# Row sums from HBM: five loads instead of six for the last rows, and the end of the sum without a second wait

## The chip, the core and the metric

The kernel runs on one NeuronCore of a Trainium2 chip. Its time is the device time of one execution in microseconds (us), taken some times on the chip; the profile of one execution goes with it. All times and profiles that are compared here ran at the full clock (1.00).

Words used below: a load *lands* when its semaphore gets the sixteenth of its sixteen increments, one from each DMA engine. The *eighth load* is the last full one (it lands near 137.8 us); the program is the same up to it in both kernels. The *last load* is the last piece of the last row. *Issue* in a chain of waits is time in which the engine waited for nothing that the profile shows; DVE is VectorE, and DVEq and SPq are the queues of VectorE and SyncE, whose semaphore and DMA instructions do not count as busy. A *paired sum* is one VectorE instruction that adds the first half of a piece to its second half and accumulates the sums.

## The reference, cut to what matters

```python
def reference(x):            # x: (32, 512, 1024) float32
    return np.sum(x, axis=-1).astype(np.float32)
```

It reads 67.1 MB and writes 64 KB.

## The kernel before

Each of 128 partitions gets 112 rows of 1024 numbers, in seven loads of 16 rows (the first cut into 1 and 15), then 16 rows more. VectorE reduces the rows; ScalarE takes six rows of the seventh tile and half of the rows of the last block. The last block is loaded in six pieces, so that little work is left when the last bytes land.

```python
BLOCKS = (112, 16); G = 16; ACT_ROWS = 6; CUT = 576
...
    def pairs_dve(xt, a, b, first, acc):
        h = (a + b) // 2
        nc.vector.tensor_tensor_reduce(
            out=xt[:, a:h], in0=xt[:, a:h], in1=xt[:, h:b], scale=1.0, scalar=first,
            op0=ADD, op1=ADD, accum_out=acc,
        )
...
    cuts = [0, 8, 12, 14, 15]          # rows: 8, 4, 2, 1, then the last row in 576 + 448
    for i, k in zip(cuts, cuts[1:]):
        nc.sync.dma_start(out=xt[:, i * D : k * D], in_=x_b[:, (c + i) * D : (c + k) * D])
    last = 15 * D
    for i, k in ((0, CUT), (CUT, D)):
        nc.sync.dma_start(out=xt[:, last + i : last + k], in_=x_b[:, c * D + last + i : c * D + last + k])

    for i, k in zip(cuts[:3], cuts[1:4]):
        h = (k - i) // 2
        rows_dve(xt, res, i, h, c + i)
        rows_act(xt, res, i + h, h, c + i + h)
    rows_act(xt, res, 14, 1, c + 14)
    pairs_dve(xt, last, last + CUT, 0.0, part)
    pairs_dve(xt, last + CUT, last + D, part, res[:, c + 15 : c + 16])
    nc.sync.dma_start(out=out_b, in_=res)
```

The second paired sum starts from the first one's sum (`part`), so it waits for two things: its load and the carried sum. The first one waits for two things too: its load, and VectorE's own semaphore. So the wait that the prediction calls write-behind-write is one behind a read, long over; it still takes a second semaphore.

## Time and profile before

| | before |
|---|---|
| time, median of the first three runs | 162.29 us (162.26 to 162.44) |
| span of the profiled execution | 160.5 us |
| VectorE busy | 76% |
| DMA, mean over the span | 418 GB/s |
| from the landing of the seventh load to that of the eighth (8.39 MB) | 19.35 us, 434 GB/s |

Three parts of the page of before (the profiler's summary of one execution): the span, the main queue (packets, MB, share of sixteen engines' span), and the chain of work that ended last, by engine:

```profile
span 160.5 us, 118 instructions
...
q1 hardware_dynamic: 2160, 67.12, 97.3%
...
DMA 74%; DVE 22%; SPq 1%; issue 0%; DVEq 0%
```

The load queue is busy for 97% of the span. The Trainium skill, "DMA: Bandwidth & Descriptors", section "Where 436 GB/s comes from", puts the ceiling of the ports at 435 GB/s, sixteen of 27.2 GB/s; the 434 GB/s above agree. The same section says that for transfers between HBM and SBUF (the on-chip memory) the HBM side, about 358 GB/s a core, binds; here, in a program on one core, it did not. Nothing but the last microseconds can be gained by moving work. This is the end of the chain of waits of before (start us, length us, what):

```profile
118.20 38.90 DMA xt<-in_x_dram
157.10 0.03 issue
157.13 0.02 DVEq L57
157.15 0.09 issue
157.24 0.46 DVE xt L57
157.70 0.02 DVE part L57
157.72 0.05 issue
157.77 0.45 DVE xt L57
158.22 0.01 DVEq L114
```

The 576-element load lands at 157.10, but the first paired sum starts at 157.24. In between lies a semaphore instruction of VectorE's queue (DVEq) of 0.02 us. The second paired sum starts at 157.77; its load landed at 157.633 by the trace, so 0.134 us go by after the last byte. The first paired sum's accumulator read ends at 157.705, 0.062 us before. The timeline of VectorE in before has both (start us, length us, engine, line, operation, operands):

```profile
157.24 0.46 DVE L57 CUSTOM_DVE_ANT_0 xt<-xt 128x288 f32<-128x288 f32 x1 [0.93 <-DMA xt<-in_x_dram]
157.62 0.08 DVE L57 DVE_READ_ACCUMULATOR2_ANT part<- 128x1 f32 x1
157.77 0.45 DVE L57 CUSTOM_DVE_ANT_0 xt<-xt,part 128x224 f32<-128x224 f32 x1
```

### The profile page before, as it was taken

Reading aid. Unit: us, or ns where it says so; the run is one execution under the profiler, and the core shown is the slowest. Engines: PE = TensorE matmul, PEld = TensorE weight load, DVE = VectorE, ACT = ScalarE, POOL = GpSimd, SP = SyncE. Lnnn points to the kernel's source line nnn. Section 1 sums busy time; section 2 is a strip of 40 time slices with the busy share of each in tenths; the row PEclk is TensorE's granted clock in tenths of the full one; section 3 lists DMA queues with packets and bytes.
Section 4 is the critical chain, followed back from the end, with each engine's and each line's share of the span. In section 5 each row is a group of like instructions: output and inputs, shape, how many; then the busy total and the mean of one; then the engine's idle time right before and its main releaser. Section 6 shows DMA issues by size and latency. Waiting matters only on the chain.

```text
span 160.5 us, 118 instructions
## 1 busy us (share of the span) xinstructions
DVE 122.7 (76%) x14; ACT 16.0 (10%) x29; POOL 0.2 (0%) x4
## 2 busy tenths in 40 slices
DVE  0000059997799959999499994999949998699992
ACT  0000000000000000000000000000000000692892
POOL 0000000000000000000000000000000000000000
DMA  9979996996996996996996996996997998999991
GB/s 376 490 306 429 490 523 261 523 523 261 523 523 261 523 523 261 523 523 261 523 523 261 523 506 278 523 506 278 523 474 310 523 425 359 392 425 425 419 401 46
DMA packets 2304, 67.18 MB, mean 418 GB/s; under 512 B 512, under 2 KB 640, under 8 KB 1024
## 3 DMA queue, kind: packets, MB, share of 16 engines
q1 hardware_dynamic: 2160, 67.12, 97.3%
q10 hardware_dynamic: 144, 0.06, 0.1%
HBM read 67.11 MB, written 0.07 MB: 418 GB/s over the span
## 4 chain that ended last, share of the span: by engine, by line
DMA 74%; DVE 22%; SPq 1%; issue 0%; DVEq 0%
DMA xt<-in_x_dram 74%; DVE res L41 21%; SPq L93 1%; DVE xt L57 1%; DVEq L57 0%; DVE part L57 0%; DVEq L114 0%
## 5 line engine op out<-in xcount | busy, mean ns | idle before, releaser
L41 DVE TENSOR_REDUCE res<-xt 128x16 f32<-128x16384 f32 (+4 forms) x10 | 121.8, 12203 | 34.5 <-DMA xt<-in_x_dram 34.5
L49 ACT ACT_TABLE_LOAD x1 | 1.3, 1283 | 137.9 <-DMA xt<-in_x_dram 137.9
L49 ACT ACTIVATE xt<-xt 128x1024 f32<-128x1024 f32 x14 | 14.6, 1042 | 3.7 <-DVE res L41 3.7
L49 ACT ACTIVATION_READ_ACCUMULATOR xt<-xt 128x1 f32 x14 | 2.6, 186 | 0.0
L57 DVE CUSTOM_DVE_ANT_0 xt<-xt 128x288 f32<-128x288 f32 x1 | 0.5, 459 | 0.9 <-DMA xt<-in_x_dram 0.9
L57 DVE CUSTOM_DVE_ANT_0 xt<-xt,part 128x224 f32<-128x224 f32 x1 | 0.5, 452 | 0.1
L151 POOL MEMSET const-uint8-127<- 128x1 uint8 x1 | 0.1, 102 | 0.0
L151 POOL MEMSET const-bfloat16-1.0<- 128x1 bf16 x1 | 0.1, 101 | 0.0
L151 POOL MEMSET const-float32-0.0<- 128x1 f32 x1 | 0.1, 98 | 0.2 <-issue 0.2
L151 POOL MEMSET const-float32-1.0<- 128x1 f32 x1 | 0.1, 98 | 0.0
L57 DVE DVE_READ_ACCUMULATOR2_ANT res<- 128x1 f32 x1 | 0.1, 84 | 0.0
L57 DVE DVE_READ_ACCUMULATOR2_ANT part<- 128x1 f32 x1 | 0.1, 83 | 0.0
## 6 DMA issues: line engine op xcount, KB each, us to landing
xt<-in_x_dram SPq DMA_DIRECT2D x1, 7680.0 KB, 21.3
xt<-in_x_dram SPq DMA_DIRECT2D x1, 4096.0 KB, 31.1
xt<-in_x_dram SPq DMA_DIRECT2D x1, 2048.0 KB, 35.7
xt<-in_x_dram SPq DMA_DIRECT2D x2, 512.0 KB, 21.1
xt<-in_x_dram SPq DMA_DIRECT2D x1, 1024.0 KB, 37.8
xt<-in_x_dram SPq DMA_DIRECT2D x1, 288.0 KB, 38.9
xt<-in_x_dram SPq DMA_DIRECT2D x1, 224.0 KB, 38.9
xt<-in_x_dram SPq DMA_DIRECT2D x6, 40.8
```

The costliest lines, as they stand in the source:

```text
L41: nc.vector.tensor_reduce(out=res[:, c : c + n], in_=xt[:, j * D : (j + n) * D].rearrange("p (j d) -> p j d", d=D), axis=X, op=ADD,)
L49: nc.scalar.activation(out=v, in_=v, func=COPY, accum_out=acc)
L57: nc.vector.tensor_tensor_reduce(out=xt[:, a:h], in0=xt[:, a:h], in1=xt[:, h:b], scale=1.0, scalar=first, op0=ADD, op1=ADD, accum_out=acc,)
L93: nc.sync.dma_start(out=xt[:, i * D : k * D], in_=x_b[:, (c + i) * D : (c + k) * D])
L151: nc = _bacc.Bacc("TRN2", target_bir_lowering=False, num_devices=1)
```

## The change

Its intent: fewer loads at the end, the last row cut nearer its middle, and a last paired sum that starts as soon as its load lands. The products get tiles of their own, so that the first paired sum waits for its load alone; a copy of one column takes the wait for the carried sum, so that the last paired sum too waits for its load alone. The diff, cut to its core:

```diff
-ACT_ROWS = 6
-CUT = 576
+ACT_ROWS = 7
+CUT = 544
...
+    seen = rpool.tile([P, 1], F32, name="seen")
+    pairs = [rpool.tile([P, D // 2], F32, name=f"pairs{i}") for i in range(3)]
...
-            out=xt[:, a:h], in0=xt[:, a:h], in1=xt[:, h:b], scale=1.0, scalar=first,
+            out=pairs[:, 0 : h - a], in0=xt[:, a:h], in1=xt[:, h:b], scale=1.0, scalar=first,
...
-    cuts = [0, 8, 12, 14, 15]
+    cuts = [0, 9, 13, 15]
...
-    for i, k in zip(cuts[:3], cuts[1:4]):
+    for i, k in zip(cuts[:2], cuts[1:3]):
         h = (k - i) // 2
         rows_dve(xt, res, i, h, c + i)
-        rows_act(xt, res, i + h, h, c + i + h)
+        rows_act(xt, res, i + h, k - i - h, c + i + h)
+    pairs_dve(xt, 13 * D, 14 * D, 0.0, res[:, c + 13 : c + 14], pairs[2])
     rows_act(xt, res, 14, 1, c + 14)
-    pairs_dve(xt, last, last + CUT, 0.0, part)
-    pairs_dve(xt, last + CUT, last + D, part, res[:, c + 15 : c + 16])
+    pairs_dve(xt, last, last + CUT, 0.0, part, pairs[0])
+    nc.vector.tensor_copy(out=seen, in_=part)
+    pairs_dve(xt, last + CUT, last + D, part, res[:, c + 15 : c + 16], pairs[1])
```

That a copy may stand in for the wait rests on the Trainium skill, "VectorE: DVE Perf Modes", section "The DRAIN you can't avoid": a value read by the next VectorE instruction can be stale, and a semaphore or one intervening VectorE instruction removes that.

More of the change, by code (lines that the diff above doesn't have):

```diff
@@ L53, in rows_act, with pairs_dve @@
             sum_act(xt[:, (j + i) * D : (j + i + 1) * D], res[:, c + i : c + i + 1])
-    def pairs_dve(xt, a, b, first, acc):
+    def pairs_dve(xt, a, b, first, acc, pairs):
         h = (a + b) // 2
         nc.vector.tensor_tensor_reduce(
-            out=xt[:, a:h], in0=xt[:, a:h], in1=xt[:, h:b], scale=1.0, scalar=first,
+            out=pairs[:, 0 : h - a], in0=xt[:, a:h], in1=xt[:, h:b], scale=1.0, scalar=first,
             op0=ADD, op1=ADD, accum_out=acc,
@@ L118 @@
     sp = mybir.EngineType.SP
+    fn = tc.nc.m.functions[0]
     entry, body = None, None
-    for blk in tc.nc.m.functions[0].blocks:
+    for blk in fn.blocks:
         ops = [i for i in blk.instructions if i.engine == sp]
```

## The prediction

> **What bounds the kernel now.** The load stream. In the chain of waits, 74% of the 160.5 us span is DMA; the tile that landed at 118.47 and the one at 137.82 are 8.39 MB apart, 434 GB/s. That is the ceiling of 435 GB/s in the Trainium skill, "DMA: Bandwidth & Descriptors", section "Where 436 GB/s comes from", so this trace agrees and the first 137 us cannot move: the diff touches nothing there. Only what follows the last bytes, and small costs at the ends of the last loads, can change.
>
> **The tail before** (timeline, semaphore landings). Landings: 8 rows 147.53, 4 rows 152.43, 2 rows 155.05, one row 156.32, 576 elements 157.10, 448 elements 157.63. First paired sum 157.24 to 157.70, its accumulator read ends 157.71; second paired sum starts 157.77, read ends 158.23, output store issued 158.29, landed 159.71, end 160.5. From the second paired sum's start, 2.7 us are fixed. It starts 0.13 us after its data. Two things hold it equally: a separate semaphore instruction of 0.02 us in front of it (the instruction waits for two semaphores), after which 0.085 us pass, and the carried sum, 0.06 us after the read. A reduction that waits for one DMA semaphore alone starts 0.024 us after the landing (137.817 to 137.841).
>
> **What the change does.**
> 1. Tiles of their own for the products take the write-behind-write wait on VectorE from the first paired sum: it needs only its load, so no semaphore instruction, 0.024 instead of 0.138 us after landing.
> 2. The copy takes the wait for the carried sum; the last paired sum then waits only for its load. The copy adds about 0.06 to 0.1 us (estimate from the 0.083 us accumulator read, also 128x1), mostly while the last load is in flight.
> 3. Five loads, not six. At 0.43 MB/us the one-row load should take 1.22 us and took 1.27, the 576 one 0.69 and took 0.78: a boundary costs 0.05 to 0.09 us. One fewer moves the last landing about 0.05 us earlier, to 157.58.
> 4. Rebalancing: 9-row reduction 9.74 us instead of 10.82, ending 147.6; 9 rows land about 148.75 instead of 147.53. ScalarE's last row (landing near 156.27) ends about 157.45, before VectorE: not critical. The 512-element paired sum (estimate 0.69 us: 0.459 for 288 elements plus 224 at the reductions' 1.05 ns each) runs 156.3 to 157.0, just in time for the 544 load at 157.01. No critical time.
>
> **Sum.** First paired sum starts about 157.04, read ends 157.49, copy 157.55 to about 157.62; last load 157.58, last paired sum starts about 157.63 rather than 157.77. With 240 elements rather than 224 (+0.02 us) the gain is about 0.12 us: span 160.38, time 162.17 us. The three runs spread 0.18 us; the range allows for that.
>
> **What would show it right or wrong.** No semaphore instruction on VectorE's queue before the paired sums, except the copy's own wait; last landing 157.5 to 157.6; last paired sum within 0.08 us after it; output issue near 158.17. If the 512-element sum delays the first piece's, step 4 is critical after all.
>
> **What would make it wrong.** A copy of over 0.15 us; the cut at 544 elements (2176 bytes, no multiple of 256), which may slow the last load; a 512-element paired sum well over 0.7 us; a slower chip. None can reach 2% (3.2 us).
>
> Predicted 162.17 us, 8 in 10 between 161.95 and 162.32; faster by over 2%: 0.01, within 2%: 0.98, slower: 0.01.

## The result

The changed kernel took 162.38 us (median of 4 runs, 162.08 to 162.57) and before 162.37 us (median of 4, 162.26 to 162.58): a ratio of 0.9997 with a 95% interval of 0.9978 to 1.0016. A ratio here is the mean time of one kernel's runs over that of the other's runs of the same rounds, so it is not quite the ratio of the medians. The time lies outside the predicted range, and the gain of 0.12 us is not to be seen. All outputs are right.

The same three parts of the page of the changed kernel:

```profile
span 160.6 us, 119 instructions
...
q1 hardware_dynamic: 2016, 67.12, 97.2%
...
DMA 75%; DVE 23%; SPq 0%; issue 0%; DVEq 0%
```

There are 144 packets fewer, one load's worth: 128 of data and 16 semaphore writes. The end of the chain of waits of the changed kernel:

```profile
117.43 39.13 DMA xt<-in_x_dram
156.55 0.02 issue
156.58 0.69 DVE pairs L59
157.27 0.01 DVE res L59
157.28 0.41 DVE pairs L59
157.69 0.02 DVE part L59
157.71 0.02 issue
157.73 0.15 DVE seen L112
157.88 0.40 DVE pairs L59
158.28 0.01 DVEq L120
```

The semaphore instruction is gone. The chain now names the copy (`seen`), with its end at 157.88 us. The timeline of VectorE in the changed kernel shows that the last sum runs since 157.82:

```profile
157.25 0.44 DVE L59 CUSTOM_DVE_ANT_0 pairs<-xt 128x272 f32<-128x272 f32 x1
157.61 0.08 DVE L59 DVE_READ_ACCUMULATOR2_ANT part<- 128x1 f32 x1
157.73 0.15 DVE L112 COPY seen<-part 128x1 f32<-128x1 f32 x1
157.82 0.47 DVE L59 CUSTOM_DVE_ANT_0 pairs<-xt,part 128x240 f32<-128x240 f32 x1
```

The last load landed at 157.792, and the last paired sum starts at 157.817, 0.025 us later, as predicted. So the wait was gained, and yet the span is longer. Adding up the two profiles by pieces, from the records of the trace, tells where it went (us):

| piece | before | changed | difference |
|---|---|---|---|
| start to the landing of the first load | 3.609 | 3.793 | +0.184 |
| to the landing of the eighth load | 134.208 | 134.209 | +0.001 |
| to the landing of the last load | 19.816 | 19.790 | -0.026 |
| to the start of the last paired sum | 0.134 | 0.025 | -0.109 |
| to the end of its accumulator read | 0.460 | 0.475 | +0.015 |
| to the issue of the store | 0.065 | 0.064 | -0.001 |
| to the store's landing | 1.421 | 1.413 | -0.008 |
| to the end of the span | 0.814 | 0.876 | +0.062 |
| sum | 160.527 | 160.645 | +0.118 |

Three rows were not foreseen. The slowest DMA engine's share of the *first* load landed 0.184 us later, where the programs are the same, and the stream never made that up. The stream's own end gained less than expected. And the end of the program after the store's landing became longer by 0.062 us.

The last of these is visible in SyncE's final checks. Before it stops, SyncE waits for every semaphore of the program, in pairs, in a fixed order. DMAs get their eight semaphores in turn. Before has 16 DMAs and its store is the sixteenth; the changed kernel has 15. Starts of SyncE's checks, from the trace (us; the store's landing is in the row of its semaphore):

| check | before | changed |
|---|---|---|
| 103 | 158.691 | 158.755 |
| 104, 101 | 158.749 | 158.813 |
| 105, 100 | 158.811 | 158.875 |
| 106, 99 | 158.875 | 159.786 (store landed at 159.769) |
| 107, 102 | 159.730 (store landed at 159.713) | 159.848 |
| 108, with the first drain | 159.795 | 159.913 |

In before the store's semaphore is in the last pair. In the changed kernel one more pair follows the landing, and a check takes 0.062 us from start to start.

### The profile page after: what moved, and what is told of

Same layout as the page of the kernel before. It is cut to its first block, busy times and chain, and to the rows that moved or that the text cites. A ratio compares the mean times of both kernels' runs of the same rounds, so it can differ in the third digit from the quotient of the medians.

```text
span 160.6 us, 119 instructions
## 1 busy us (share of the span) xinstructions
DVE 121.5 (76%) x16; ACT 17.2 (11%) x31; POOL 0.2 (0%) x4
## 4 chain that ended last, share of the span: by engine, by line
DMA 75%; DVE 23%; SPq 0%; issue 0%; DVEq 0%
DMA xt<-in_x_dram 75%; DVE res L43 21%; DVE pairs L59 1%; SPq L95 0%; DVE seen L112 0%; DVE part L59 0%; DVE res L59 0%; DVEq L120 0%
## 5 line engine op out<-in xcount | busy, mean ns | idle before, releaser
L43 DVE TENSOR_REDUCE res<-xt 128x16 f32<-128x16384 f32 (+3 forms) x9 | 119.8, 13309 | 36.5 <-DMA xt<-in_x_dram 36.5
L51 ACT ACTIVATE xt<-xt 128x1024 f32<-128x1024 f32 x15 | 15.6, 1044 | 2.4 <-DMA xt<-in_x_dram 2.3
L59 DVE CUSTOM_DVE_ANT_0 pairs<-xt 128x512 f32<-128x512 f32 (+1 forms) x2 | 1.1, 567 | 0.2 <-DMA xt<-in_x_dram 0.2
L59 DVE CUSTOM_DVE_ANT_0 pairs<-xt,part 128x240 f32<-128x240 f32 x1 | 0.5, 468 | 0.0
```

Of the source, the lines that this page charges most:

```text
L43: nc.vector.tensor_reduce(out=res[:, c : c + n], in_=xt[:, j * D : (j + n) * D].rearrange("p (j d) -> p j d", d=D), axis=X, op=ADD,)
L51: nc.scalar.activation(out=v, in_=v, func=COPY, accum_out=acc)
L59: nc.vector.tensor_tensor_reduce(out=pairs[:, 0 : h - a], in0=xt[:, a:h], in1=xt[:, h:b], scale=1.0, scalar=first, op0=ADD, op1=ADD, accum ...
```

## The experiments

The theory after this first look has four parts. **A**: the late first landing is chance of one execution, and hides the gain in the times. **C**: the end lost 0.062 us to the turn of the semaphores. **Waits**: own tiles and copy are worth about 0.11 us. **F**: a load costs each engine a fixed amount, so five are cheaper than six. The rivals: **B** or **H**, the late start belongs to the changed kernel (B: every time by the same lag; H: on the whole); **D**, the end's length is chance; **E**, the waits gain nothing; **F2**, the stream gains by the cut, not by the number of loads.

### b_same, a_same: both kernels again

No edit.

> The kernel before, unchanged, timed against itself. Theory A (the 0.185 us by which the slowest DMA engine lands later, from the first load on, is chance of one execution): its times spread by 0.2 us or more, ratio 1.000 within 0.002; in the profile the gap from the first to the sixteenth landing of the 137.8 us load can be anything from 0.3 to 0.7 us; the paired sum still starts 0.13 us after the last landing, and the last load lands 19.82 us after the eighth. Rival B (the lag belongs to the changed kernel): the gap is 0.28 us again, as in the first profile of before.

> The changed kernel again. Theory A: the same local tail as in its first profile whatever the lag: last paired sum 0.025 us after the last landing, end of the span 0.88 us after the output store's landing against 0.82 in before; ratio to before near 0.9996 and not resolved from 1; the gap of first to sixteenth landing differs from the 0.695 us of its first profile. Rival B: the gap is 0.69 us again and the ratio is 1.000 for that reason.

Before against itself: 162.21 against 162.20 us, ratio 1.0000 (0.9988 to 1.0012). The changed kernel: 162.25 against 162.20 us, ratio 1.0000 (0.9988 to 1.0012). The sixteen runs of before, its eleven and the five of b_same, reach from 162.06 to 162.52 us, so one execution differs from the next by up to 0.46 us, several times the effect. The gap from the first to the sixteenth increment of the eighth load, 0.280 us in the first profile of before and 0.695 in that of the changed kernel, was 0.460 in b_same and 0.461 in a_same: B falls, and H is left for the last experiment. The Trainium skill, "DMA: Bandwidth & Descriptors", section "Why a DMA increments its semaphore by 16 and not by 1", says that the engines of one DMA finish independently; this is that, and the load is done when the slowest is.

In a_same the last paired sum again starts 0.024 us after the last landing and the end takes 0.875 us after the store's landing, so both local findings repeat. The time does not move by anything that can be resolved, as theory A expects (0.9996 lies within the interval); but its own mean was 0.01 us over that of before, so this alone shows no gain.

### a_out_last: the store's semaphore moved back by an extra load

```diff
-            parts = (0, 1, m) if done + c == 0 else (0, m)
+            parts = (0, 1, 8, m) if done + c == 0 else (0, m)
```

> The changed kernel with the first tile cut once more (rows 1 to 7 and 8 to 15), so that there are 16 transfers, as before, and the output store again has the semaphore that the end of the kernel checks last. Theory C (the end lost 0.062 us because another semaphore is checked after the store's): the end of the span comes 0.82 us after the store's landing, not 0.88, and from the last load's landing to the end it takes 2.79 us against 2.85 in the changed kernel and 2.90 in before. Rival D (the 0.06 us is chance of the end): still 0.88.

From the store's landing to the end it took 0.813 us, and from the last landing to the end 2.789, as theory C expects. The time was 162.15 against 162.20 us, ratio 0.9997 (0.9984 to 1.0011): no gain that can be resolved. The extra load is not free. A packet usually takes 8 to 9 ns beyond its bytes at the 27.2 GB/s of one port: 611 ns for 16,384 bytes (602 by the rate), 159 for 4,096 (151), 25 for 448 (16.5). A load has eight data packets and a semaphore write of 9 ns on each engine, so an estimate from these is 8 x 8.4 + 9 = 0.076 us for each additional load, and this edit pays that to gain 0.062.

### w_only: the waits alone, on the loads of before

```diff
+    seen = rpool.tile([P, 1], F32, name="seen")
+    pairs = [rpool.tile([P, D // 2], F32, name=f"pairs{i}") for i in range(2)]
...
-            out=xt[:, a:h], in0=xt[:, a:h], ...
+            out=pairs[:, 0 : h - a], in0=xt[:, a:h], ...
...
-    pairs_dve(xt, last, last + CUT, 0.0, part)
-    pairs_dve(xt, last + CUT, last + D, part, res[:, c + 15 : c + 16])
+    pairs_dve(xt, last, last + CUT, 0.0, part, pairs[0])
+    nc.vector.tensor_copy(out=seen, in_=part)
+    pairs_dve(xt, last + CUT, last + D, part, res[:, c + 15 : c + 16], pairs[1])
```

> The kernel before with its six loads and its cut at 576, and only the new tiles and the copy. From the durations of the two profiles: no semaphore instruction before the first paired sum, which starts 0.025 us after its landing; carried sum, copy (start 0.035 us after the read, and the last sum 0.086 us after the copy's start) make the last paired sum start 0.08 us after the last landing, between before (0.13) and after (0.025). End of the span 2.84 us after the last landing against 2.90. Rival E (the whole gain of the tail comes from the loads, none from the waits): 0.13 us and 2.90.

The timeline of VectorE in this run:

```profile
157.50 0.08 DVE L59 DVE_READ_ACCUMULATOR2_ANT part<- 128x1 f32 x1
157.62 0.15 DVE L109 COPY seen<-part 128x1 f32<-128x1 f32 x1
157.69 0.44 DVE L59 CUSTOM_DVE_ANT_0 pairs<-xt,part 128x224 f32<-128x224 f32 x1
```

The last load landed at 157.595, so the last sum starts 0.094 us after it (expected 0.08), and from the last landing to the end it takes 2.833 us (2.84 expected, 2.90 in before). E falls: the waits gain by themselves. The cut at 576 leaves the copy as what is waited for: it starts 0.022 us after the last landing, and the sum 0.072 us after the copy's start, before the copy's 0.153 us are over. With the cut at 544 the copy started 0.061 to 0.086 us before the landing in all runs of the changed kernel and of a_eight below, while the sum stayed at 0.024 to 0.026 us after the landing. So there it is the load that is waited for, although the chain names the copy. The time was 162.19 against 162.20 us, ratio 1.0004 (0.9992 to 1.0017), which resolves nothing.

### a_nocopy: the changed kernel without the copy

```diff
-    nc.vector.tensor_copy(out=seen, in_=part)
```

> The changed kernel without the copy, so that the last paired sum waits for load and carried sum itself. Theory: a semaphore instruction before it again, start 0.13 us after the last landing instead of 0.024, last landing to end 2.97 us instead of 2.857. Rival (the copy is not needed, its own 0.15 us cancels it): 0.03 us.

```profile
157.42 0.08 DVE L59 DVE_READ_ACCUMULATOR2_ANT part<- 128x1 f32 x1
157.71 0.47 DVE L59 CUSTOM_DVE_ANT_0 pairs<-xt,part 128x240 f32<-128x240 f32 x1 [0.21 <-DMA xt<-in_x_dram]
```

The last load landed at 157.581 and the carried sum was read by 157.50, long ready, and yet the sum starts at 157.714, 0.133 us after the load. From the last landing to the end it took 2.971 us, 0.11 more than the changed kernel's 2.86. So the loss is not the wait for the carried sum itself. It is the second semaphore, whose wait comes as an instruction of its own in front of the sum. The own tiles are still there in this run, so by themselves they gave nothing at the end: 2.971 is the 2.894 of before, 0.016 for the longer sum and 0.061 for the check that the next runs move. The copy without own tiles was not run. The Trainium skill, "Perfetto Trace Analysis", section "Identifying Dependency Chains", says that an instruction waiting on several engines may get EventSemaphore instructions in front of it; here that costs 0.11 us after the landing.

### a_idle1, a_idle5: the store's semaphore moved by idle transfers of one element

```diff
+    idle = rpool.tile([1, 1], F32, name="idle")        # a_idle5: [1, 5], range(5)
+    for i in range(1):
+        nc.scalar.dma_start(out=idle[:, i : i + 1], in_=x_flat[0:1, i : i + 1])
+
     full = C - G
```

> The changed kernel with one more transfer of a single element (4 bytes, one partition, issued by ScalarE at the start, never used): it shifts the semaphores by one, so that the store has again the one checked last, and unlike the extra cut of a_out_last it costs the load stream next to nothing. Theory C: last landing to end 2.79 us (2.857 in the changed kernel, 2.897 in before), and the last load lands 19.68 us (mean of 16 engines) after the eighth, as in a_same. If only chance hides the gains of stream and end, its mean lies 0.2 us below that of before, to within 0.08; rival H (the changed kernels lose at the start of the stream what they gain at its end): within 0.1 us of before again, with a first load that lands later.

> The same with five such transfers: the store then has the semaphore that is checked first, with four more checks after it. Theory C: each check after the landing costs 0.062 us, so store landing to end takes 0.814 + 4 x 0.062 = 1.06 us and last landing to end 3.04 us; time 0.25 us over a_idle1. Rival D (the end's length has nothing to do with the checks): 0.81 or 0.88.

From the store's landing to the end: 0.814 us with one idle transfer, 0.876 in the changed kernel, 1.059 with five. One check less saves 0.062 us, and three checks more cost 0.183. From the last landing to the end: 2.796 and 3.041 us, as expected to 0.01 us. Theory C holds and D falls. The time of a_idle1 was 162.16 against 162.44 us, ratio 0.9985 (0.9972 to 0.9997); that of a_idle5 162.45 against 162.44 us, ratio 1.0008 (0.9995 to 1.0022). The 0.06 us between the changed kernel and a_idle1 is below what these times can tell, but the 0.25 us between a_idle1 and a_idle5 is not: their means are 162.19 and 162.52 us, five runs each.

### a_rowsplit, b_cut544: what the stream gains from

```diff
-    cuts = [0, 9, 13, 15]          # a_rowsplit, from the changed kernel
+    cuts = [0, 9, 13, 14, 15]
```

```diff
-CUT = 576                          # b_cut544, from before
+CUT = 544
```

> The changed kernel with rows 13 and 14 of the last block in two loads, so six loads again, all else equal. Theory F (a load costs each DMA engine 9 packets x 8.5 ns = 0.076 us, whatever its size): the last load lands 19.76 us after the eighth (mean of engines), not 19.68. Rival F2 (the stream gained from the cut at 544): 19.68. The last paired sum starts 0.025 us after the last landing either way, and the end takes 2.79 us, as there are 16 transfers.

> The kernel before with the last row cut at 544 instead of 576. Theory F (the stream's 0.14 us comes from the number of loads): the last load lands 19.82 us after the eighth (mean of engines), as in before; the two pieces take 1.32 us together. Rival F2 (part of it comes from the cut): 19.76, the two pieces 1.27 us. Tail as in before: the last paired sum starts 0.13 us after the last landing.

Here the mean landing over the sixteen engines is used, since the latest of them adds its own chance. In before the last load lands 19.819 and 19.826 us after the eighth (two profiles), in a_same 19.675.

a_rowsplit landed at 19.824, not 19.76, but it was already 0.095 us later than a_same at the nine-row load (11.003 against 10.908, see below). From that load on it took 8.821 us against 8.767: the extra load costs 0.054 us (0.047 to 0.075 against the nine profiles of the changed kernel and its relatives with 9, 4 and 2 rows), under the estimate of 0.076 in all of them. b_cut544 landed at 19.772, not at 19.82, and its two pieces together took 1.265 us: the cut alone gains 0.05 us. So F and F2 both hold. Together they make 0.10 of the 0.14 us by which a_same lands earlier than before; the remaining 0.04 is not assigned by any run. Why 544 and 480 elements go through faster than 576 and 448 stays open. In the profiles it is not the packets' own time that differs: eight packets of each piece and two semaphore writes make 1.354 us in before (93 and 74 ns a packet) and 1.354 in the changed kernel (88 and 79). In b_cut544 the last paired sum starts 0.134 us after the landing, as in before.

### a_eight_idle1, a_eight, b_nine: the nine-row load

The first profile of the changed kernel had not gained at the last landing: by the mean of the engines 19.828 us, as before. The nine-row load itself was late: it landed 11.072 us after the eighth, and 10.908 in a_same. Its packets of 36,864 bytes, usually 1.364 us, took up to 1.568.

```diff
-    cuts = [0, 9, 13, 15]          # a_eight from the changed kernel, a_eight_idle1 from a_idle1
+    cuts = [0, 8, 13, 15]
```

```diff
-    cuts = [0, 8, 12, 14, 15]      # b_nine, from before
+    cuts = [0, 9, 12, 14, 15]
...
-        rows_act(xt, res, i + h, h, c + i + h)
+        rows_act(xt, res, i + h, k - i - h, c + i + h)
```

> a_idle1 with loads of 8, 5 and 2 rows before the cut row instead of 9, 4 and 2. In the profiles so far the packets of 36,864 bytes (nine rows) of five of seven kernels took up to 0.2 us longer than their usual 1.364 us at about 138 to 143 us, which put the mean landing of that load 0.0 to 0.16 us late; the packets of 32,768 bytes (eight rows) never did in three profiles. Theory S (it is the nine-row load): no packet of the first load of this block over 1.25 us (usual 1.213), last load 19.68 us after the eighth, last landing to end 2.79 us; time 0.2 to 0.25 us below before. Rival S2 (the stall belongs to that time of the program or to chance): some packets of 1.25 to 1.4 us, last load 19.75 to 19.85 us after the eighth.

> The changed kernel with loads of 8, 5 and 2 rows instead of 9, 4 and 2, without the idle transfer. Theory S: no slow packets, last load 19.68 us after the eighth, last landing to end 2.857 us, time 0.17 us below before and 0.06 over a_eight_idle1 (inside the noise). Rival S2: as above.

> The kernel before with six loads of 9, 3, 2, 1 rows, 576 and 448 elements, the waits untouched. Theory S: packets of 36,864 bytes over 1.40 us between 138 and 143 us, and a last load up to 0.16 us later than 19.82 us after the eighth (chance may spare it, as in two of seven). Rival S2 (the changed kernel's other differences bring the stall): none, 19.82. Tail as in before.

With eight rows, the packets of that load (32,768 bytes, usually 1.213 us) took at most 1.213 us in a_eight, and in a_eight_idle1 at most 1.249 but for one of 128, which took 1.279; the last load landed at 19.69 us in both. b_nine has the waits and tiles of before and a nine-row load, and its packets took up to 1.526 us; its last load landed at 19.876. So the slow packets come with the nine-row load, and not with the other differences of the changed kernel. Of the eleven profiles with a nine-row load, nine have packets over 1.40 us, and the load's mean landing is 0.00 to 0.16 us late; of the seven without, one has a single packet over 1.25 us in that place. Why a packet of nine rows is slow there is not settled: the five-row packets of a_eight, usually 0.761 us, took up to 0.885 and those of its sibling's repetition 0.929, so it is not only nine rows. Over all eighteen profiles, of the packets of the last block with 9, 5, 3 or 1 rows, 162 of 2816 took over 0.04 us more than usual, and of those with 8, 4 or 2 rows 2 of 4864; whether the odd number is what matters, no run was made to test. The packets of sixteen rows (65,536 bytes, usually 2.42 us) have slow ones too, 199 of 13,824, up to 2.575 us.

b_nine was clumsy: it gives ScalarE nine rows of the last block, not eight, so that the store waits for ScalarE and is issued 1.095 us after the last landing (0.66 in before). Its single time, 162.74 us, says nothing of the load.

The time of a_eight_idle1 was 162.10 against 162.27 us, ratio 0.9987 (0.9973 to 1.0000), that of a_eight 162.31 against 162.27 us, ratio 0.9994 (0.9981 to 1.0007).

### a_again1 to a_again3, a_eight_idle1_again: is the start late by chance?

No edit: the changed kernel three times, and a_eight_idle1 once more. These are runs for what was still open: a_same had shown no gain in its times.

> The changed kernel, unchanged. Chance theory: from the eighth load's landing to the end 22.54 us when the nine-row load does not stall and up to 22.66 when it does, against 22.68 to 22.71 in before; the landing of the eighth load anywhere from 137.7 to 138.2, as in before. Over the fifteen timed runs of the three copies the mean lies 0.05 to 0.15 us below that of before of this call. Rival H (the changed kernel starts its stream later): the mean within 0.03 us of before, the eighth load's landing above 137.85 in most profiles.

> A second copy of the same, for the mean of the three and for one more profile of the first landing and of the nine-row load. Chance theory: mean of the three 0.05 to 0.15 us below before; rival H: within 0.03 us of before.

> A third copy of the same, for the same mean and one more profile. Chance theory: mean of the three 0.05 to 0.15 us below before; rival H: within 0.03 us of before.

> The version with loads of 8, 5 and 2 rows and the idle transfer again: 22.47 us from the eighth load's landing to the end, mean 0.2 us below before, to within 0.08. Rival H: within 0.1 us of before.

| run | this, median us | before, median us | ratio (95%) |
|---|---|---|---|
| a_again1 | 162.28 | 162.46 | 0.9993 (0.9980 to 1.0007) |
| a_again2 | 162.27 | 162.46 | 0.9986 (0.9974 to 0.9999) |
| a_again3 | 162.28 | 162.46 | 0.9986 (0.9974 to 0.9999) |
| a_eight_idle1_again | 162.18 | 162.46 | 0.9987 (0.9975 to 1.0000) |

The fifteen runs of the changed kernel have a mean of 162.277 us, the nine of before 162.472: 0.195 us less, with a standard error of 0.052 from the two spreads. On this chip the changed kernel is faster, by a little more than was expected. The first call had shown 0.04 us less (means of four and four runs) and the second 0.01 more (five and eleven). Weighting the three by their standard errors (about 0.13, 0.08 and 0.05, from the spreads of the runs) gives some 0.12 us less, with an error of 0.04; the second and the third differ by about two of their errors. H is not needed to explain the first results: its clear mark, a mean within 0.03 us of before, did not come back. Its other mark did: the eighth load landed at 137.945 to 137.975 in these three profiles, above 137.85. There is no profile of before from this call to compare with, but the table below has the same mark: in the five profiles of before and the kernels made from it the eighth load landed at 137.70 to 137.82, and in nine of the thirteen of the changed kernel and its relatives later than in any of these. The times speak against a lasting delay of that size. They are the span plus 1.78 to 1.80 us in all eighteen profiles, so with 22.70 us from the eighth load to the end the runs of before, 162.06 to 162.76 us in all calls, would have had it at about 137.6 to 138.3 (an estimate), as widely spread as the whole column of the table. And the 0.12 us less is within 0.02 us of the 0.139 that the pieces after the eighth load give below, which leaves the changed kernel a later start of 0.02 us, with an error of 0.04. So chance is enough to explain the first two profiles; a start later by some hundredths in the changed kernel is not excluded.

All profiles together, in us (*mean* is over the sixteen engines; ScalarE's lateness in b_nine is in its last two columns):

| kernel | eighth load lands | to the last landing | the same, mean | last sum starts after it | last landing to end | eighth to end |
|---|---|---|---|---|---|---|
| before | 137.817 | 19.816 | 19.819 | 0.134 | 2.894 | 22.710 |
| b_same | 137.779 | 19.780 | 19.826 | 0.134 | 2.900 | 22.680 |
| b_cut544 | 137.701 | 19.732 | 19.772 | 0.134 | 2.904 | 22.636 |
| b_nine | 137.815 | 19.817 | 19.876 | 0.135 | 3.327 | 23.144 |
| w_only | 137.796 | 19.799 | 19.811 | 0.094 | 2.833 | 22.632 |
| changed | 138.002 | 19.790 | 19.828 | 0.025 | 2.853 | 22.643 |
| a_same | 137.803 | 19.680 | 19.675 | 0.024 | 2.861 | 22.541 |
| a_again1 | 137.951 | 19.682 | 19.690 | 0.024 | 2.855 | 22.537 |
| a_again2 | 137.945 | 19.689 | 19.698 | 0.025 | 2.861 | 22.550 |
| a_again3 | 137.975 | 19.650 | 19.724 | 0.024 | 2.859 | 22.509 |
| a_nocopy | 137.738 | 19.843 | 19.772 | 0.133 | 2.971 | 22.814 |
| a_rowsplit | 138.172 | 19.750 | 19.824 | 0.024 | 2.792 | 22.542 |
| a_out_last | 138.019 | 19.660 | 19.685 | 0.024 | 2.789 | 22.449 |
| a_idle1 | 138.194 | 19.690 | 19.692 | 0.024 | 2.796 | 22.486 |
| a_idle5 | 137.813 | 19.686 | 19.681 | 0.024 | 3.041 | 22.727 |
| a_eight | 137.694 | 19.670 | 19.692 | 0.026 | 2.861 | 22.531 |
| a_eight_idle1 | 137.849 | 19.671 | 19.688 | 0.025 | 2.801 | 22.472 |
| a_eight_idle1_again | 137.845 | 19.737 | 19.735 | 0.026 | 2.801 | 22.538 |

The first column, where the programs do the same (but for the extra cut in a_out_last and the idle transfers), has a range of 0.50 us. The column of the last landing to the end repeats to within 0.01 us for each program. From the eighth landing to the end the five profiles of the changed kernel have a mean of 22.556 us, the two of before 22.695: 0.139 us less, of which 0.100 lie before the last landing (19.698 against 19.798) and 0.039 after it (2.858 against 2.897).

A version that beats before: a_eight_idle1, 0.21 us below it by the means in both of its calls (162.118 against 162.329, 162.258 against 162.472), about 0.13% (each call's interval just reaches 1; the two together exclude it). Against the changed kernel it is not resolved: on the chip of the last call 162.258 against 162.277.

## Why the prediction was wrong, and where it was right

- **"What bounds the kernel now": right.** The load stream, at 434 GB/s.
- **"the first 137 us cannot move": this step failed.** The change does not touch them, but they move from one execution to the next: the eighth load landed anywhere from 137.69 to 138.19 us. In the two profiles that were compared first, this alone made 0.185 us, more than the predicted gain. The span that the prediction started from was one such draw. The range took a spread of 0.18 us of three runs as that of the kernel. Sixteen runs spread by 0.46, and the medians of before went from 162.20 to 162.46 us by call. A range of 0.2 us to either side was too narrow for a gain of 0.12, and a time of 162.38 fell out of it without the kernel being at fault. Of the 0.21 us between 162.17 and 162.38, 0.08 is before's own level (162.37, not 162.29), and the rest is about the gain, which four runs with a standard error of 0.13 could not show. That the median fell outside is in part bad luck: in the four later sets of five runs the same kernel had 162.25, 162.28, 162.27 and 162.28, all inside, with before at 162.20 and 162.46. What the lateness starts with is seen, not explained: single packets of 4,096 bytes of the first load took up to 1.005 us in before and 0.828 in the changed kernel, against usually 0.159 (at most 0.287 in the one-row load of before), and the longer one was in the profile that started earlier.
- **Steps 1 and 2 (tiles and copy): right.** The last sum starts 0.024 us after its load. The copy was mis-sized, 0.153 us instead of 0.06 to 0.1, which is past the 0.15 that the prediction named as a danger. It did no harm: the next instruction can start 0.072 us after the copy's start (w_only), and with the cut at 544 the copy starts early enough.
- **Step 3 (loads): right in kind, mis-sized.** Predicted 0.05 us, measured 0.100 over the five profiles of the changed kernel and the two of before. One load fewer gives 0.054 us (a_rowsplit), the cut another 0.05 (b_cut544), which the prediction had feared as a loss. The nine-row load gives up to 0.16 us of it back in some executions, in the first profile all of it. The prediction had no such term.
- **Step 4 (no critical time in the new split of rows): right.** The 512-element sum took 0.692 us (0.69 predicted), and ScalarE was never last in the changed kernel.
- **"From the second paired sum's start, 2.7 us are fixed": this step failed too.** The end grew by 0.062 us, because fifteen DMAs leave the store with another semaphore than sixteen do.
- **The sum.** Predicted -0.12 us; the pieces after the eighth load measure -0.139 (-0.100 loads, -0.110 wait, +0.016 longer sum, +0.061 end, and some thousandths for the store). Terms that were missed in both directions nearly cancel: the loads and the wait gave more than predicted, and the checks at the end took some of it back. That the sum agrees with the predicted 0.12 is therefore partly luck. The times together give about -0.12.

## What to carry to other kernels

When a gain is a tenth of a per cent, cut the profile into pieces between landings and compare the pieces: those behind the last landing repeated to 0.01 us here and the end of the stream to 0.14, while the whole time needed some fifteen runs beside nine to show 0.2 us. Before the last bytes of a stream are used, give the instruction that waits for them one semaphore only, and let an earlier instruction of the same engine take the other waits. Count what a change does to the number of DMAs, since a different count may hand the last store a semaphore that is checked before others, and 0.062 us for each check that follows.

## What the Trainium skill lacked or had wrong

- "Perfetto Trace Analysis", section "Identifying Dependency Chains", says that EventSemaphore instructions may be inserted, but not what they cost: 0.11 us from the landing to the start (0.133 with, 0.024 without, a_nocopy and the changed kernel).
- "DMA: Bandwidth & Descriptors", section "Why small descriptors are slow (HBM only)", gives a fixed overhead of about 3 cycles a packet and 32 bytes of descriptors for each operation: together 4.7 ns, an estimate from the page with the 850 MHz and the 27.2 GB/s of its bandwidth section. The traces show about 8 to 9 ns (medians) for packets of 448 to 61,440 bytes, beyond their bytes at 27.2 GB/s.
- No page tells that the slowest of the sixteen engines can be late from the first load on and stay so: the first load's increments lay 0.30 to 0.92 us apart, and the eighth load's 0.28 to 0.77.
- No page tells that some load sizes bring slow packets in the middle of a full stream: 36,864 bytes took up to 1.578 us instead of 1.364, with packets over 1.40 in nine of eleven profiles.
- No page tells of the order of the checks at the end of a program, 0.062 us each, and that a store's landing may be followed by one to five of them.
